# A hybrid decoder block on one core: the next unit's first block product one segment earlier in the down projection

## The chip, the cores and the metric

The program runs on one core of a Trainium2 chip. The core has a matrix engine (PE, with its weight loads shown apart as PEld), a vector engine (DVE), a scalar engine (ACT), a general engine (POOL) and a synchronisation engine (SP); SP and POOL issue the transfers between the chip's memory and the core's SBUF. The matrix engine writes its sums to PSUM, which is divided into banks. The metric is the device time of one execution in microseconds (us); shorter is better.

## The reference

One layer of a decoder block on 512 positions of width 2048, in float32. The part that matters here is the gated MLP at its end: `w_ffn_in` has 2 x 5632 columns, `w_ffn_out` 5632 rows and 2048 columns.

```python
def conv_ffn(h, w_ffn_in, conv_w, conv_b, w_ffn_out):
    S = h.shape[1]
    up = h @ w_ffn_in
    a, b = up[..., :D_FF], up[..., D_FF:]
    a_pad = jnp.pad(a, ((0, 0), (CONV_W - 1, 0), (0, 0)))
    a = (conv_w[0] * a_pad[:, 0:S] + conv_w[1] * a_pad[:, 1:S + 1]
         + conv_w[2] * a_pad[:, 2:S + 2] + conv_b)
    return (jax.nn.gelu(a, approximate=True) * b) @ w_ffn_out
```

Before it come two norms, an input projection, gated linear attention, differential attention and an output projection; after it a norm and a residual sum.

## The kernel before

**Precision.** Each float32 matrix is split into a rounded part (hi) and the rest (lo), and a product is formed as hi x hi + hi x lo + lo x hi, three matmuls. For weights the split is done on the fly. One *granule* is 128 x 1024 weights (512 KB): ACT copies it to hi (line 138), DVE subtracts hi from it to get lo (line 139), and PE reads both. In the down projection the three matmuls stand in lines 1400, 1401 and 1402, in the up projection in lines 1298, 1299 and 1300. The hi and lo pieces lie in a `ring` of three pairs; from the second unit of the down projection on every fourth granule goes to a spare pair `xhi`, `xlo` instead. A piece can be written again only when PE has read it.

**Seven products.** The large projections multiply blocks of 2 x 2 with seven products where the plain way needs eight. A *unit* is one such set of seven, and each product is a *segment* of two granules. A segment of the down projection has 2 x 12 = 24 matmuls of 512 columns. The segments are called x0, z0, y0, z1, x1, y1, y2. The weights that they multiply are:

- x0: block (0,0), loaded by SP into two `rt` buffers, here called t. When x0's split has read t, POOL issues a transfer that *adds* block (0,1) to it in place (`more`, line 1246; line 1506 in the stretch that is ordered by hand).
- z0: t after that addition.
- y0: t after DVE has added block (1,1), called b22, to it (line 1263).
- z1: b22, loaded by SP into `raw` buffers; POOL then adds to it in place in the same way.
- x1: block (1,0), called b21.
- y1: b22 after the addition.
- y2: t after DVE has added b21 to it (line 1281).

The other factor of each product, made of activations, is called a11, s5, s2, s3, a12, s7 and a22 in the same order. For the down projection it is stored in memory by the up projection, loaded by SP into a buffer `st`, and split by ACT (line 151) and DVE (line 152) into its place in `ah` and `al`: this is `prepare`.

**Banks.** x0, y0, y1 and y2 add up in the same PSUM banks (two, one for each 128 rows of output, called j0 and j1 here); after each of them its running sum is read out into the result `acc` by DVE (line 1408) or, in the first two units, partly by ACT (line 1406). z0 and z1 share two other banks, x1 has its own. A later matmul into a bank has to wait until the read of what stands there is done.

**The units.** The up projection has 20 units (plus the first pairs of columns, done plainly), the down projection 10, called d0 to d9 here: five pairs of row groups (index c) by two halves of the columns (cb). Units with an even number start a new c, for which seven new activation factors are prepared. The last row group is done plainly at the end, together with the final norm.

**What sets the order.** From the last three segments of the last up unit to y2 of d0 the order is written out by hand: `change_over` gives the list of segments, `run_in_order` walks through it, makes the granules two or three ahead of their matmuls, and runs hooks (`at`, `prepare_at`) behind each granule. ACT, DVE, PE and POOL keep that order among themselves. From z0 of d1 on, the loop over `downs` states the segments, and a list scheduler in the build, which works with its own estimates of durations, sets the order of the instructions on each engine; it may place an instruction ahead of one that stands earlier in the code. Each engine then works through its own list strictly in order, and so does SP with its transfers. In the loop, x0 of the next unit stands between y1 and y2 of the present one.

Of the kernel before, what the change touches and what calls it, by code (L numbers as in the profile page):

```python
# [35 lines left out]
def hybrid_layer(ctx: ExitStack, tc: tile.TileContext, x, attn_pre_norm, w_in, w_alpha_up, b_alpha,  # L36
# [10 lines left out]
    def dma(o, i):  # L47
        return nc.sync.dma_start(out=o, in_=i)
# [51 lines left out]
    def load(src, a, by=None):  # L100
        raw = wpool.tile([P, GR], F32, name="raw", tag="raw", bufs=4)
        (by or nc.sync).dma_start(out=raw.rearrange("p (a b) -> p a b", a=a), in_=src)
        return raw
# [46 lines left out]
    def split(hi, lo, src):  # L150
        act(hi, src, AF.Copy)  # L151
        tt(lo, src, hi.bitcast(F32), ALU.subtract)
# [10 lines left out]
    def bcast_row(tile_ap, row):  # L163
        dma(tile_ap, row.partition_broadcast(P))
# [960 lines left out]
    def small_tile(name, dt=F32):  # L1125
        return fp.tile([P, GR], dt, name=name, tag="t4", bufs=6)

    def large_tile(name, dt=F32):
        return fp.tile([P, D], dt, name=name, tag="t8", bufs=6)
# [82 lines left out]
    def load_t(src, a):  # L1212
        raw = rp.tile([P, GR], F32, name="rt", tag="rt", bufs=4)
        dma(raw.rearrange("p (a b) -> p a b", a=a), src)
        return raw
# [170 lines left out]
    def piece(v, t, h):  # L1386
        return v[:, t, HK * h:HK * (h + 1), :].rearrange("p k c -> p (k c)")

    def prepare(c, n):
        raw = small_tile("st")  # L1390
        dma(raw, sd[c][n].rearrange("p g x -> p (g x)"))
        split(piece(ah, *place[n]), piece(al, *place[n]), raw)
# [17 lines left out]
    def down_unit(c, cb):  # L1410
        def block(i, j, g):
            gi = 2 * c + 1 + g
            col = 1024 * cb + 512 * j
            return w_y3[:, 4 * gi + 2 * i:4 * gi + 2 * i + 2, col:col + 512]

        def chain(ch):
            return [bank(psa if ch == "y" else psm) for _ in range(2)]

        def out(seg, b):
            for j in range(2):  # L1420
                half, col, sign = {"x0": (0, 0, 1), "z0": (1, 1, 1), "y0": (0, 1, -1), "z1": (0, 1, 1), "x1": (0, 0, 1),
                                   "y1": (1, 1, -1), "y2": (1, 0, 1)}[seg]
                sl = slice(1024 * cb + 512 * col, 1024 * cb + 512 * (col + 1))
                into(acc[2 * half + j][:, sl], b[j], sign, c == 0 and seg in ("x0", "z0", "y0", "y2"))

        return Unit(2, block, down_prods, chain, out, joined=True)
# [21 lines left out]
    downs = [down_unit(c, cb) for c in range(NG // 2) for cb in range(2)]  # L1448
# [4 lines left out]
    def at(u, seg, g, *fs):  # L1453
        hooks.setdefault((u, seg, g), []).extend(fs)

    def load_unit(u):
        u.t = [load_t(u.block(0, 0, g), u.a) for g in range(2)]
        u.b22, u.b21 = [], []

    def load_b(u, name, i, j, by=None):  # L1460
        getattr(u, name).extend(load(u.block(i, j, g), u.a, by) for g in range(2))

    def add_t(u, name, g):
        tt(u.t[g], u.t[g], getattr(u, name)[g], ALU.add)

    def prepare_parts(c, n):
        got = []

        def first():
            got.append(small_tile("st"))  # L1470
            dma(got[0], sd[c][n].rearrange("p g x -> p (g x)"))

        def second():
            split(piece(ah, *place[n]), piece(al, *place[n]), got[0])

        return first, second

    def prepare_at(c, n, load_at, split_at):
        f, g = prepare_parts(c, n)
        at(*load_at, f)  # L1480
        at(*split_at, g)
# [40 lines left out]

    def change_over(u):
        d0, d1 = downs[:2]
        order = [(u, "x1"), (u, "y1"), (d0, "x0"), (u, "y2")]
        order += [(d0, g) for g in ("z0", "y0", "z1", "x1", "y1")] + [(d1, "x0"), (d0, "y2")]
        at(u, "x1", 1, late_tiles)
        prepare_at(0, "s2", (u, "x1", 0), (u, "y1", 0))
        prepare_at(0, "s3", (u, "x1", 1), (d0, "x0", 0))
        prepare_at(0, "s7", (u, "y1", 1), (u, "y2", 0))  # L1530
        prepare_at(0, "a12", (d0, "x0", 0), (d0, "z0", 0))
        prepare_at(0, "a22", (u, "y2", 0), (d0, "y0", 0))
        at(u, "x1", 1, lambda: (add_t(u, "b21", 0), add_t(u, "b21", 1)))
        at(u, "x1", 0, lambda: load_unit(d0))
        at(u, "x1", 0, lambda: load_b(d0, "b22", 1, 1))
        at(u, "y1", 1, lambda: load_b(d0, "b21", 1, 0))
        at(d0, "z0", 1, lambda: load_unit(d1))
        for g in range(2):
            at(u, "y2", g, lambda g=g: add_t(d0, "b22", g))
        at(d0, "z1", 0, lambda: add_t(d0, "b21", 0))  # L1540
        at(d0, "x1", 0, lambda: add_t(d0, "b21", 1))
        for where in ((d0, "z0", 0), (d0, "y0", 0), (d0, "z1", 0), (d0, "x1", 0)):
            at(*where, lambda: late_sums.pop(0)())
        return order

    order = change_over(ups[-1])
    u = ups[-1]
    u.b21 = [load(u.block(1, 0, g), u.a) for g in range(2)]
    for n in ("a11", "s5"):
        prepare(0, n)  # L1550
    with tc.manual_schedule(engines=IN_ORDER):
# [4 lines left out]
    for i, u in enumerate(downs):  # L1556
        if i == 0:
            continue
        nxt = downs[i + 1] if i + 1 < len(downs) else None
        nc_ = (i + 1) // 2  # L1560
        first = i % 2 == 0
        last_cb = i % 2 == 1 and nxt is not None

        if first:
            prepare(i // 2, "s3")
        if i == 6:
            g3 = large_tile("g3")
            bcast_row(g3, ffn_post_norm[0])
        u.y0()
        if first:  # L1570
            prepare(i // 2, "a12")
        u.z1()
        if first:
            prepare(i // 2, "s7")
        u.x1()
        if first:
            prepare(i // 2, "a22")
        if last_cb:
            prepare(nc_, "a11")
        u.y1()  # L1580
        if last_cb:
            prepare(nc_, "s5")
        if nxt is not None:
            nxt.x0()
        if last_cb:
            prepare(nc_, "s2")
        u.y2()
        if nxt is not None:
            nxt.z0()
# [119 lines left out]
```

## Time and profile before

| | us |
|---|---|
| median of 3 runs | 2089.43 |
| lowest and highest | 2087.04 and 2091.67 |
| the profiled execution's own time | 2090.44 |
| its span, first to last instruction | 2088.7 |
| PE busy in the span | 2053.1 |
| DVE busy in the span | 1502.4 |
| ACT busy in the span | 993.8 |
| first matmul of the down projection | 1631.4 from the span's start |

The profile was taken on one execution. Times in views are microseconds from the start of its span. "Busy" of PE counts a matmul until its modelled end, which lies behind the start of the next one, so short pauses do not show in it; the starts of successive matmuls tell more. A row of the timeline gives start, duration, engine, line, operation, what is written and read, and in brackets how long the engine sat idle before it and what ended that.

### The profile page before, as it was taken

The numbers are of one execution on the slowest core, as the hardware profiler recorded it, in microseconds if no ns is written. First come the engines' busy times: TensorE is split into PE (matmuls) and PEld (weight loads), VectorE is DVE, ScalarE is ACT, GpSimd is POOL, SyncE is SP. The second block draws the span as 40 slices with busy tenths as digits, with TensorE's granted clock in tenths as the row PEclk, the third lists the DMA queues.
The fourth block names the chain that finished last, engine by engine and source line by source line (L and its number), as shares of the span: only waits on it lengthen the run. The fifth ranks groups of instructions, "written<-read, shape, count | busy, mean of one in ns | idle before, by whom it ended". The sixth has DMA issues, their size and how long they took to land.

```text
span 2088.7 us, 35508 instructions
## 1 busy us (share of the span) xinstructions
PE 2053.1 (98%) x14417; PEld 1893.3 (91%) x14417; DVE 1502.4 (72%) x1790; ACT 993.8 (48%) x1301; POOL 290.4 (14%) x306
## 2 busy tenths in 40 slices
PE   7999999999999999999999999999999999999997
PEld 6799999999988889899999999999999878787786
DVE  5967777666762265977767777678677778888877
ACT  5544444555552243454454455455455544444443
POOL 0112222222200000011111110111111011111100
PEclk9999999999999999999999999999999999999999
DMA  5488887888883354367577676775777876775753
GB/s 211 124 185 187 196 193 175 192 182 209 193 265 106 93 190 147 98 151 183 133 169 179 143 166 167 163 165 148 187 162 171 249 201 156 198 190 156 180 163 141
DMA packets 281465, 358.61 MB, mean 172 GB/s; under 512 B 14848, under 2 KB 223156, under 8 KB 279380
## 3 DMA queue, kind: packets, MB, share of 16 engines
q1 hardware_dynamic: 192148, 259.85, 37.3%
q0 software_dynamic: 84800, 94.38, 29.9%
q10 hardware_dynamic: 4352, 2.10, 0.4%
q8 instruction: 113, 1.85, 0.3%
q14 instruction: 52, 0.43, 0.1%
HBM read 311.72 MB, written 44.56 MB: 171 GB/s over the span
## 4 chain that ended last, share of the span: by engine, by line
PE 61%; issue 28%; DMA 4%; DVE 3%; POOL 2%; ACT 1%; POOLq 0%; DVEq 0%; SPq 0%; ACTq 0%
PE bank L1300 8%; PE bank L1299 7%; PE bank L1298 7%; PE bank L192 3%; PE bank L193 3%; PE bank L194 3%; PE bank L793 3%; PE bank L795 3%; PE bank L794 3%; PE bank L797 3%; PE bank L798 2%; PE bank L799 2%; PE bank L176 1%; PE bank L174 1%; PE bank L175 1%
## 5 line engine op out<-in xcount | busy, mean ns | idle before, releaser
L138 ACT ACTIVATE ring<-raw 128x1024 fp32r<-128x1024 f32 x315 | 333.1, 1060 | 516.5 <-PE bank L1299 114.1
L139 DVE TENSOR_TENSOR ring<-raw,ring 128x1024 fp32r<-128x1024 f32 x315 | 383.0, 1222 | 270.9 <-ACT ring L138 269.8
L1300 PE MATMUL bank<-ah,ring 128*128 128x256 f32 x1280 | 354.0, 277 | 0.6 <-DVE ring L139 0.5
L1298 PE MATMUL bank<-ah,ring 128*128 128x256 f32 x1280 | 353.9, 276 | 0.0
L1299 PE MATMUL bank<-al,ring 128*128 128x256 f32 x1280 | 353.8, 276 | 0.0
L138 ACT ACTIVATE ring<-rt 128x1024 fp32r<-128x1024 f32 x221 | 233.0, 1059 | 244.0 <-PE bank L1299 135.1
L139 DVE TENSOR_TENSOR ring<-rt,ring 128x1024 fp32r<-128x1024 f32 x221 | 268.7, 1221 | 90.7 <-ACT ring L138 87.3
L1300 PEld LDWEIGHTS bank<-ah,ring 128*128 128x128 f32 x1280 | 240.4, 188 | 1.0 <-DVE ring L139 1.0
L1299 PEld LDWEIGHTS bank<-al,ring 128*128 128x128 f32 x1280 | 240.4, 188 | 0.1
L1298 PEld LDWEIGHTS bank<-ah,ring 128*128 128x128 f32 x1280 | 240.4, 188 | 0.1
L1401 PE MATMUL bank<-ring,ah 128*128 128x512 f32 x424 | 166.6, 393 | 6.7 <-DVE ring L139 6.7
L1402 PE MATMUL bank<-ring,al 128*128 128x512 f32 x424 | 165.4, 390 | 0.0
L1400 PE MATMUL bank<-ring,ah 128*128 128x512 f32 x424 | 158.9, 392 | 0.7 <-ACT ring L138 0.7
L193 PE MATMUL bank<-ring,ah 128*128 128x512 f32 x280 | 109.5, 392 | 0.0
L192 PE MATMUL bank<-ring,ah 128*128 128x512 f32 x280 | 109.4, 396 | 0.0
L194 PE MATMUL bank<-ring,al 128*128 128x512 f32 x280 | 109.1, 392 | 0.0
L1246 POOL DMA_DIRECT2D raw<-in_w_ffn_in_dram x40 | 51.2, 1309 | 398.6 <-DVE ring L139 398.6
L1401 PEld LDWEIGHTS bank<-ring,ah 128*128 128x128 f32 x424 | 79.6, 188 | 27.2 <-DVE ring L139 11.0
L1400 PEld LDWEIGHTS bank<-ring,ah 128*128 128x128 f32 x424 | 79.4, 188 | 19.9 <-ACT ring L138 3.6
L1246 POOL DMA_DIRECT2D rt<-in_w_ffn_in_dram x40 | 51.0, 1295 | 325.3 <-DVE ring L139 302.8
L1402 PEld LDWEIGHTS bank<-ring,al 128*128 128x128 f32 x424 | 79.7, 188 | 16.2
L797 PE MATMUL bank<-ring,ah 128*128 128x256 f32 x320 | 92.0, 288 | 1.9 <-ACT ah L151 1.9
(358 smaller groups left out, 5651.8 us busy)
## 6 DMA issues: line engine op xcount, KB each, us to landing
raw<-in_w_ffn_in_dram SPq DMA_DIRECT2D x96, 512.0 KB, 4.8
raw<-in_w_in_dram SPq DMA_DIRECT2D x56, 512.0 KB, 4.4
raw<-in_w_ffn_out_dram SPq DMA_DIRECT2D x48, 512.0 KB, 6.7
raw<-in_w_in_dram POOLq DMA_DIRECT2D x40, 512.0 KB, 7.1
rt<-in_w_ffn_in_dram SPq DMA_DIRECT2D x40, 512.0 KB, 6.5
rt<-in_w_ffn_in_dram POOLq DMA_DIRECT2D x40, 512.0 KB, 6.2
raw<-in_w_ffn_in_dram POOLq DMA_DIRECT2D x40, 512.0 KB, 6.8
raw<-in_w_o_dram SPq DMA_DIRECT2D x32, 512.0 KB, 4.0
```

Source lines behind the costliest of these rows:

```text
L138: act(hi, raw, AF.Copy)
L139: tt(lo, raw, hi.bitcast(F32), ALU.subtract)
L192: mm(banks[t], ah[:, t, s, :], w[0][:, k, :], start=st, stop=False)
L193: mm(banks[t], ah[:, t, s, :], w[1][:, k, :], start=False, stop=False)
L194: mm(banks[t], al[:, t, s, :], w[0][:, k, :], start=False, stop=sp)
L797: mm(o, sh[:, n, kk, :], wh[:, k, :], start=st, stop=False, **NOW)
L1298: mm(o, wh, sh[:, :, kk, :], start=start and kk == 0 and n == 0, stop=False, **NOW)
L1299: mm(o, wh, sl[:, :, kk, :], start=False, stop=False, **NOW)
L1300: mm(o, wl, sh[:, :, kk, :], start=False, stop=kk == HK - 1, **NOW)
L1400: mm(b[j], sh[:, o:o + P], w[0][:, q, :], start=start and st == 0, stop=False, **NOW)
L1401: mm(b[j], sh[:, o:o + P], w[1][:, q, :], start=False, stop=False, **NOW)
L1402: mm(b[j], sl[:, o:o + P], w[0][:, q, :], start=False, stop=st == 3, **NOW)
```

## The change

The segment x0 of the next unit moves from between y1 and y2 to between x1 and y1. This is done in the loop for every unit, and by hand in the change from the up projection to the down projection (there d0's x0 also moves ahead of the last up unit's y1, and d1's x0 ahead of d0's y1). The hooks that load and split the activation factors move with it, the load of d0's first weights is written ahead of the stretch that is ordered by hand, a11 of the next c is prepared one segment sooner, s5 of the next c ahead of x0 and not behind y1, and a22 between x0 and y1 and not ahead of y1. No instruction is added or taken away.

```diff
@@ def change_over(u):
-        order = [(u, "x1"), (u, "y1"), (d0, "x0"), (u, "y2")]
-        order += [(d0, g) for g in ("z0", "y0", "z1", "x1", "y1")] + [(d1, "x0"), (d0, "y2")]
+        order = [(u, "x1"), (d0, "x0"), (u, "y1"), (u, "y2")]
+        order += [(d0, g) for g in ("z0", "y0", "z1", "x1")] + [(d1, "x0"), (d0, "y1"), (d0, "y2")]
         at(u, "x1", 1, late_tiles)
-        prepare_at(0, "s2", (u, "x1", 0), (u, "y1", 0))
-        prepare_at(0, "s3", (u, "x1", 1), (d0, "x0", 0))
+        prepare_at(0, "s2", (u, "x1", 0), (d0, "x0", 1))
+        prepare_at(0, "s3", (u, "x1", 1), (u, "y1", 0))
...
-        at(u, "x1", 0, lambda: load_unit(d0))
...
     u.b21 = [load(u.block(1, 0, g), u.a) for g in range(2)]
+    load_unit(downs[0])
...
         u.y0()
         if first:
             prepare(i // 2, "a12")
+        if last_cb:
+            prepare(nc_, "a11")
         u.z1()
         if first:
             prepare(i // 2, "s7")
         u.x1()
-        if first:
-            prepare(i // 2, "a22")
-        if last_cb:
-            prepare(nc_, "a11")
-        u.y1()
         if last_cb:
             prepare(nc_, "s5")
         if nxt is not None:
             nxt.x0()
+        if first:
+            prepare(i // 2, "a22")
+        u.y1()
         if last_cb:
             prepare(nc_, "s2")
         u.y2()
         if nxt is not None:
             nxt.z0()
```

The change moves instructions on every engine from there on. Three places of it are shown; rows are instructions in the order in which an engine takes them, with line, operation, tile written, tiles read and size.

**ACT, where the up projection goes over into the down projection.** `raw_16738/16740` are the last up unit's x1, `raw_16620/16622` its y1, `rt_16442/16444` its y2; `rt_16785/16787` before, and `rt_16742/16744` in the change, are d0's t. Before:

```order
L138 ACTIVATE ring_84<-raw_16740 128x1024
L138 ACTIVATE ring_84<-raw_16620 128x1024
L138 ACTIVATE ring_84<-raw_16622 128x1024
L138 ACTIVATE ring_84<-rt_16785 128x1024
L151 ACTIVATE ah_79<-st_16783 128x1024
L138 ACTIVATE ring_84<-rt_16787 128x1024
L138 ACTIVATE ring_84<-rt_16442 128x1024
```

The same place in the change:

```order
L138 ACTIVATE ring_84<-raw_16740 128x1024
L138 ACTIVATE ring_84<-rt_16742 128x1024
L138 ACTIVATE ring_84<-rt_16744 128x1024
L138 ACTIVATE ring_84<-raw_16620 128x1024
L138 ACTIVATE ring_84<-raw_16622 128x1024
L1406 ACTIVATE acc0_16825<-bank_16833 128x512
L1406 ACTIVATE acc1_16826<-bank_16834 128x512
L151 ACTIVATE ah_79<-st_16788 128x1024
L138 ACTIVATE ring_84<-rt_16442 128x1024
```

The two splits of d0's x0 change places with the two of the last up unit's y1; y2 of the up unit now follows its y1 with no other segment between.

**ACT, in the loop, at the end of d3.** `raw_17765/17767` is d3's y1, `rt_17665/17667` before and `rt_17629/17631` in the change its y2; `rt_17909/17911` before and `rt_17877/17879` in the change are t of d4. Before:

```order
L138 ACTIVATE xhi_17036<-raw_17835 128x1024
L138 ACTIVATE ring_84<-raw_17765 128x1024
L151 ACTIVATE ah_79<-st_18013 128x1024
L138 ACTIVATE ring_84<-raw_17767 128x1024
L138 ACTIVATE ring_84<-rt_17909 128x1024
L151 ACTIVATE ah_79<-st_18053 128x1024
L138 ACTIVATE xhi_17036<-rt_17911 128x1024
L138 ACTIVATE ring_84<-rt_17665 128x1024
```

The same place in the change:

```order
L138 ACTIVATE xhi_17036<-raw_17839 128x1024
L138 ACTIVATE ring_84<-rt_17877 128x1024
L151 ACTIVATE ah_79<-st_18013 128x1024
L138 ACTIVATE ring_84<-rt_17879 128x1024
L138 ACTIVATE ring_84<-raw_17765 128x1024
L151 ACTIVATE ah_79<-st_18053 128x1024
L138 ACTIVATE xhi_17036<-raw_17767 128x1024
L138 ACTIVATE ring_84<-rt_17629 128x1024
L138 ACTIVATE ring_84<-rt_17631 128x1024
L138 ACTIVATE ring_84<-rt_17877 128x1024
```

x0's two splits of d4 stood behind both splits of y1, and now stand ahead of them, right behind x1's second one. The last row is already z0 of d4.

**DVE and PE, in the change, around y2 of d3.** `bank_17633/17634` are j0 and j1 of d3's shared banks, `bank_17881/17882` those of d4, `bank_17981/17982` z0 of d4. DVE:

```order
L139 TENSOR_TENSOR ring_84<-rt_17629,ring_84 128x1024
L1408 TENSOR_TENSOR acc0_16825<-acc0_16825,bank_17881 128x512
L1408 TENSOR_TENSOR acc1_16826<-acc1_16826,bank_17882 128x512
L139 TENSOR_TENSOR ring_84<-rt_17631,ring_84 128x1024
L139 TENSOR_TENSOR ring_84<-rt_17877,ring_84 128x1024
L1408 TENSOR_TENSOR acc2_16823<-acc2_16823,bank_17633 128x512
L1263 TENSOR_TENSOR rt_17877<-rt_17877,raw_18017 128x1024
L1408 TENSOR_TENSOR acc3_16824<-acc3_16824,bank_17634 128x512
```

PE, the last matmuls of y1 of d3 and what follows them:

```order
L1402 MATMUL bank_17634<-xhi_17036,al_80 128x512
L1400 MATMUL bank_17981<-ring_84,ah_79 128x512
L1400 MATMUL bank_17982<-ring_84,ah_79 128x512
L1401 MATMUL bank_17981<-ring_84,ah_79 128x512
```

PE does not go from y1 to y2 of d3, though the code states them so: the scheduler puts the whole first granule of d4's z0 (12 matmuls) between them. Then come 12 matmuls of y2 into j0, two of z0's second granule, y2's 12 into j1, and the rest of z0. DVE reads y1's sum out of j0 and j1 (the last L1408 rows) behind the split of that first granule of z0, and between the two stands the addition of b22 to t.

## The prediction

> **What bounds the kernel now.** First the page: PE is busy in 98% of the span, so I read PE.
>
> ```profile
> span 2088.7 us, 35508 instructions
> PE 2053.1 (98%) x14417; PEld 1893.3 (91%) x14417; DVE 1502.4 (72%) x1790; ACT 993.8 (48%) x1301; POOL 290.4 (14%) x306
> ```
>
> The change begins near 1620 us, so all else is left as it is, and the question is what PE loses from there to the end of the down projection. "Busy" hides that. I cut the stretch at the starts of segments, in the view by windows (window, length, PE busy with its matmuls, PEld with its weight loads, then DVE, ACT, POOL, clock, share of the DMA engines, GB/s).
>
> ```profile
> 1642.45:1656.38 13.93, 12.18 (x51) 8.79 (x49) 13.43 (x13) 9.55 (x12) 1.26 (x2) 1.00 0.83 292
> 1678.18:1692.06 13.88, 11.95 (x50) 8.86 (x48) 7.51 (x8) 7.28 (x10) 0.00 (x0) 1.00 0.73 189
> 1708.38:1715.39 7.01, 5.99 (x25) 4.43 (x24) 4.89 (x6) 4.88 (x6) 1.17 (x1) 1.00 0.86 325
> 1726.27:1737.93 11.66, 11.46 (x49) 8.87 (x48) 9.77 (x10) 7.83 (x9) 1.04 (x1) 1.00 0.35 126
> 1803.29:1816.99 13.70, 11.90 (x49) 8.78 (x48) 13.26 (x15) 6.97 (x7) 0.79 (x1) 1.00 0.38 129
> 1816.99:1882.30 65.31, 65.31 (x289) 54.02 (x288) 53.41 (x58) 28.15 (x28) 8.66 (x8) 1.00 0.76 192
> 1882.30:1895.86 13.56, 11.79 (x50) 8.86 (x48) 12.89 (x15) 6.97 (x7) 0.81 (x1) 1.00 0.36 125
> 1955.70:1973.10 17.40, 16.77 (x71) 12.91 (x70) 16.57 (x19) 8.27 (x9) 0.36 (x1) 1.00 0.41 111
> 1973.10:2027.52 54.42, 54.42 (x241) 45.08 (x240) 44.33 (x49) 21.72 (x21) 6.76 (x6) 1.00 0.66 165
> ```
>
> The rows of 288 and 240 weight loads show PE undisturbed: 54.42 / 240 = 0.2267 us a matmul, so 2.72 us a granule and 5.44 us a segment. The clock is full everywhere. The other rows hold two segments each (10.88), the third row one (5.44), the one at 1955.70 three (16.32). They lose:
>
> - d0's z0 and y0: 13.93 - 10.88 = 3.05
> - d0's y2 and d1's z0: 13.88 - 10.88 = 3.00
> - d1's y1: 7.01 - 5.44 = 1.57
> - z0 and y0 of d2, d4, d6: 0.78, 2.82, 2.68
> - d7's y2, d8's z0 and y0: 17.40 - 16.32 = 1.08
>
> Together 14.98 us. Nothing else in the stretch loses more than 0.1. This is all that any reordering of it can win.
>
> Who is late? PE's own waits name the splits, and behind the splits, in ACT's waits (engine, tile, line, releaser: us in total, times, longest), stands a transfer:
>
> ```profile
> PE bank L1401 <- DVE ring L139: 6.7, 9, 1.0
> ACT ring L138 <- DMA rt<-in_w_ffn_out_dram: 59.0, 16, 9.0
> ACT xhi L138 <- DMA rt<-in_w_ffn_out_dram: 12.7, 4, 4.3
> ```
>
> `rt` is t, and the transfer is the addition that POOL issues behind x0 and that z0 needs. ACT and then POOL, in order of time:
>
> ```profile
> 1641.09 1.06 ACT L138 ACTIVATE ring<-rt 128x1024 fp32r<-128x1024 f32 x1 [3.33 <-DMA rt<-in_w_ffn_out_dram]
> 1645.08 1.06 ACT L138 ACTIVATE ring<-rt 128x1024 fp32r<-128x1024 f32 x1 [1.99 <-DMA rt<-in_w_ffn_out_dram]
> 1683.07 1.06 ACT L138 ACTIVATE ring<-rt 128x1024 fp32r<-128x1024 f32 x1 [9.02 <-DMA rt<-in_w_ffn_out_dram]
> 1687.06 2.01 ACT L138 ACTIVATE ring<-rt 128x1024 fp32r<-128x1024 f32 x2 [1.01 <-DMA rt<-in_w_ffn_out_dram]
> 1788.13 1.06 ACT L138 ACTIVATE ring<-raw 128x1024 fp32r<-128x1024 f32 x1 [5.19 <-DMA raw<-in_w_ffn_out_dram]
> 1801.49 1.06 ACT L138 ACTIVATE ring<-rt 128x1024 fp32r<-128x1024 f32 x1 [6.42 <-DMA rt<-in_w_ffn_out_dram]
> 1805.45 1.06 ACT L138 ACTIVATE xhi<-rt 128x1024 fp32r<-128x1024 f32 x1 [2.90 <-DMA rt<-in_w_ffn_out_dram]
> ```
>
> ```profile
> 1630.58 1.17 POOL L1506 DMA_DIRECT2D rt<-in_w_ffn_out_dram  x1 [14.21 <-DVE ring L139]
> 1632.85 1.19 POOL L1506 DMA_DIRECT2D rt<-in_w_ffn_out_dram  x1 [1.10 <-DVE ring L139]
> 1672.77 1.18 POOL L1506 DMA_DIRECT2D rt<-in_w_ffn_out_dram  x1 [15.25 <-DVE ring L139]
> 1675.10 1.19 POOL L1506 DMA_DIRECT2D rt<-in_w_ffn_out_dram  x1 [1.15 <-DVE ring L139]
> 1791.89 1.17 POOL L1246 DMA_DIRECT2D rt<-in_w_ffn_out_dram  x1 [11.81 <-DVE ring L139]
> 1795.35 1.19 POOL L1246 DMA_DIRECT2D rt<-in_w_ffn_out_dram  x1 [2.29 <-DVE xlo L139]
> ```
>
> From issue to the split that waited for it: 10.5 and 12.2 us at d0, 10.3 and 12.0 at d1, 9.6 and 10.1 at d4. From the start of x0 to the start of z0 PE needs two segments, 10.88 us. The additions are issued at about the start of x0 (d4: x0 at 1803.29 - 10.88 = 1792.41, issue at 1791.89), and the split takes ACT 1.06 and DVE 1.2 more. So the stall is a race of about 10 us against 10.9 - 2.0 = 8.9.
>
> **The change, part by part.** No instruction is added, so engine time is not the matter; waits are.
>
> *The hand-written stretch, d0.* Two rows of DVE show when the granules behind x1 are split there now; they are y1's, and the change puts x0's in their place.
>
> ```profile
> 1621.73 1.23 DVE L139 TENSOR_TENSOR ring<-raw,ring 128x1024 fp32r<-128x1024 f32 x1 [0.29 <-ACT ring L138]
> 1624.45 1.23 DVE L139 TENSOR_TENSOR ring<-raw,ring 128x1024 fp32r<-128x1024 f32 x1 [1.50 <-ACT ring L138]
> ```
>
> x0's additions are then issued at about 1623.0 and 1625.7, not 1630.58 and 1632.85. With the same 10.5 and 12.2 us they land at 1633.5 and 1637.9, and z0's granules are wanted on ACT at about 1640 and 1643. The 3.05 go (y0's share too: its additions on DVE stand behind z0's splits). Bounds: 2.2 (z0 alone) to 3.05.
>
> *The hand-written stretch, d1.* Now z0 starts late, by ACT first:
>
> ```profile
> 1684.18 0.50 PE L1400 MATMUL bank<-ring,ah 128*128 128x512 f32 x1 [0.40 <-ACT ring L138]
> ```
>
> In the change x0 is one segment ahead of y1, and z0's first granule comes 10.88 us behind x0, hardly less than the 11.4 of now (d0's y2 starts at 1678.18, x0 5.44 ahead of it at 1672.74, z0 at 1684.18). What moves is the issue: now x0's split waits on ACT behind y1's second granule and its transfer; in the change only the ring's slot holds it, which z1's first granule gives back about 8 us ahead of x0. I take 4 us earlier, more than the 3.00 lost: they go. Bounds 1.2 (only the second granule, which gets 2.72 us more because PE puts y2 ahead of it) to 3.00.
>
> *d1's y1.* Its granule waited for the addition behind z1. It now comes one segment later, 5.44 against 1.57 lost: 1.57 go.
>
> *The loop.* On PE z0's first granule now stands ahead of y2, so from x0 to z0 it is again two segments, 10.88 us. On that count alone the change gives nothing. The win is in ACT's queue: at d3 x0 of d4 stands behind the split of y1's second granule, which sat 5.19 us for its transfer until 1788.13. In the change x0's split comes ahead of it. Its slot is that of z1's first granule, free some 5 us into z1; ACT 1.06 and DVE 1.22 later the addition goes out, 7.5 us from z1's start and 3.4 us ahead of x0's start, where now it is 0.5. With 9.6 us it lands 6.2 us after x0's start against the 8.9 wanted. z0's second granule gains 2.72 us more. So 0.78 + 2.82 + 2.68 + 1.08 = 7.36 go. Bounds: 3 (the issue no earlier, only the second granules gain) and 7.36.
>
> *Added: the eviction.* y2 adds into the banks that y1's sum is read from. In the up unit nothing is between them any more, so PE waits for line 1331.
>
> ```profile
> 1625.99 0.28 PE L1298 MATMUL bank<-ah,ring 128*128 128x256 f32 x1
> 1626.19 0.69 DVE L1329 TENSOR_TENSOR u<-bank,p 128x512 f32<-128x512 f32 x1 [0.51 <-PE bank L1300]
> 1632.47 0.68 DVE L1331 TENSOR_TENSOR u<-u,bank 128x512 f32<-128x512 f32 x1
> 1642.18 1.22 DVE L139 TENSOR_TENSOR ring<-rt,ring 128x1024 fp32r<-128x1024 f32 x1 [4.36 <-ACT ring L138]
> 1643.46 0.50 PE L1401 MATMUL bank<-ring,ah 128*128 128x512 f32 x1 [0.62 <-DVE ring L139]
> ```
>
> y1's first matmul starts at 1625.99, and DVE took up the read of x1 at 1626.19, 0.2 us later; the read lasts 0.68; PE follows DVE's end by 0.06 (1642.18 + 1.22 to 1643.46). That is 0.94, or 2.2 with one split of 1.22 in front. I take 1.0, once. In the loop z0's first granule, 2.72 us, covers the two reads of 0.68 and the 1.22 between them (0.68 + 1.22 + 0.68 = 2.58), and j1 is wanted another 3 us later: 0 there, and 0.9 each for nine units if the cover goes.
>
> The Trainium skill (PSUM — Partial Sum Buffer, section on bank collisions) says the same as the build does here, that PSUM is to be guarded by whole banks and not by addresses. By that rule y2 cannot start on the half that is already read. It leaves the 1.0 as it is and is why the cover in the loop matters.
>
> *b22 and the loads.* The `raw` buffers of the next unit's b22 are those of b21, which no y1 holds, so they are not later. The next b21's are y1's and come 5.4 us later, with three segments and more to spare: 0. a22 is needed a segment behind its place but its buffer and split come far ahead: 0.
>
> *Sum.* 3.05 + 3.00 + 1.57 + 7.36 = 14.98 off, 1.0 on. For residues that I can't place (z0's first granule stays the tightest, nine times) I leave 1.5. Net -12.5: span 2088.7 - 12.5 = 2076.2. Outside the span that execution had 2090.44 - 2088.7 = 1.74, so 2077.9; the median of the runs lies 1.0 below that execution. Forecast 2077.
>
> **The rivals.**
>
> *Half of it.* z0's first granule stays late as its distance on PE is the same; the lower bounds hold: 2.2 + 1.2 + 1.57 + 3 - 2.2 = 5.8 off, 2083.6. For it: PE's new order. Against it: ACT's queue.
>
> *No change.* The transfers are the limit and the waits come back at y1, y0 or the loads. For it: 0.83 to 0.86 of the DMA engines are taken in two of the rows that lose. Against it: 0.35 to 0.41 in four others, and no loss in the row with 0.76. About 2089.
>
> *Slower.* In the change the additions behind z1 and behind x0 go out a segment apart where there were two, with the loads of the next unit among them. If the addition behind x0 takes 3 us longer, z0's first granule is late at every unit, and PE, in order, holds y2 behind it too. The point is a landing later than 8.9 us after x0's start: with the issue 3.4 ahead, 12.3 us; with the issue as now, 9.4. At 15.5 us each of nine boundaries pays 3.2, 29 in all against 15: 2089.4 + 29 - 15 + 1 = 2104; at 14.5, 2095. For it: 12.0 was seen once; against it: 9.6 to 10.1 in the loop.
>
> The Trainium skill (DMA: Bandwidth & Descriptors, section SWDGE vs HWDGE vs iDMA) has each DMA engine take its queues in turn, POOL's among SP's. By that a transfer put among more others lands later, which is this rival's step; no row here shows by how much.
>
> **How the numbers follow.** Forecast 0.64 (2074 to 2081), half 0.17, no change 0.10, slower 0.09. The forecast's own range goes from all 14.98 won with nothing on (2088.7 - 14.98 + 1.74 - 1.0 = 2074.5) to 2081, where half of the loop's 7.36 stays. The 80% range reaches over the half to 2086.5, and down to 2073 since the runs shown spread by 2 us about their median. A difference under 0.2%, 4.2 us, can't be told from no change: the line lies at 2085.25. Faster 0.81, same 0.11, slower 0.08.
>
> **What would show it.** In the new trace the additions behind x0 should be issued 3 to 4 us ahead of x0's first matmul, not 0.5; ACT's wait for `rt` from memory should shrink from 59.0 + 12.7 and PE's for line 139 from 6.7; d0's z0 and y0 should take 10.9, and between the up unit's y1 and y2 there should be one new pause of about 1 us with line 1331 behind it. The prediction is wrong if PE stops at z0's first granule with transfers of 12 us and more, or before y2 with line 1408 behind it.

## The result, and the profile after

The changed kernel takes 2078.03 us (median of 6 runs, 2076.67 to 2079.63) against 2088.78 for the kernel before (6 runs, 2086.67 to 2092.32): a ratio of 0.9944, 95% interval 0.9932 to 0.9956. Forecast were 2077, a range of 2073 to 2086.5, and 0.81 for faster. Ten more runs of the same kernel, made later beside experiments, had medians of 2080.3 and 2080.1; over all 16 the median is 2078.9.

The page of the changed kernel, its span and its engines:

```profile
span 2075.0 us, 35488 instructions
PE 2047.0 (99%) x14417; PEld 1893.9 (91%) x14417; DVE 1507.1 (73%) x1790; ACT 1000.0 (48%) x1301; POOL 290.2 (14%) x306
```

The stretch from the up unit's x1 to the end of the down projection, first of the kernel before, then of the changed one (the view by windows, columns as in the prediction):

```profile
1620.55:2032.96 412.41, 403.31 (x1823) 329.94 (x1822) 337.09 (x354) 190.97 (x198) 47.33 (x40) 1.00 0.70 188
```

```profile
1618.42:2019.84 401.42, 398.03 (x1826) 331.38 (x1824) 340.74 (x354) 196.17 (x198) 47.33 (x40) 1.00 0.71 193
```

The second window holds two weight loads more (1824 against 1822), two matmuls of 0.2267 us. So for the same work the stretch gave 412.41 - 401.42 + 0.45 = 11.44 us. The span fell by 13.7; the other 2.3 lie outside the stretch (it begins 2.13 sooner), in work that the change leaves alone. One execution's span says little about that work: in two later traces of the changed kernel the stretch begins at 1624.53 and 1619.47, and takes 0.6 us more and 0.2 less. Cut at the places that lost before, again by windows:

```profile
1629.39:1636.54 7.15, 5.65 (x50) 5.49 (x48) 5.34 (x6) 5.44 (x6) 0.00 (x0) 1.00 1.03 388
1642.07:1653.32 11.25, 11.25 (x50) 8.86 (x49) 11.25 (x12) 8.09 (x10) 1.26 (x2) 1.00 0.74 250
1675.14:1685.79 10.65, 10.65 (x48) 8.82 (x47) 8.34 (x9) 5.62 (x7) 1.17 (x1) 1.00 0.88 277
1707.55:1712.99 5.44, 5.44 (x25) 4.50 (x24) 3.74 (x6) 2.12 (x2) 0.00 (x0) 1.00 1.06 335
1685.79:1941.47 255.68, 255.68 (x1129) 211.71 (x1128) 220.56 (x232) 126.68 (x126) 31.90 (x27) 1.00 0.71 190
1941.47:1949.12 7.65, 5.75 (x25) 4.42 (x24) 7.65 (x9) 3.07 (x3) 0.00 (x0) 1.00 0.48 147
1949.12:2019.84 70.72, 70.72 (x314) 58.58 (x312) 56.68 (x61) 28.45 (x27) 7.11 (x6) 1.00 0.57 147
```

d0's z0 and y0 (second row) take 11.25 where they took 13.93; d0's y2 and d1's z0 (third) 10.65 where they took 13.88 (the window holds 47 matmuls, one short of two segments, and 47 by 0.2267 is 10.65: nothing is lost); d1's y1 (fourth) 5.44 where it took 7.01. The fifth row is 47 segments in one piece, from d1's y0 to d7's y1: 1128 matmuls by 0.2267 are 255.7, so nothing is lost in it. Besides the 0.37 of the second row two rows still lose: the first, the up unit's y1 (7.15 - 5.44 = 1.71), and the sixth, around d8's z0 (7.65 - 5.44 = 2.21). The waits name both, and ACT's waits no longer contain `rt` from `w_ffn_out` at all; what ACT now waits for most in the down projection is PE:

```profile
PE bank L1401 <- DVE ring L139: 1.9, 1, 1.9
PE bank L1298 <- DVE u L1331: 1.5, 1, 1.5
ACT ring L138 <- PE bank L1402: 123.9, 79, 3.5
```

POOL's rows for the additions behind x0 of d4, d5 and d6, in order of time:

```profile
1774.58 1.17 POOL L1246 DMA_DIRECT2D rt<-in_w_ffn_out_dram  x1 [4.55 <-DVE ring L139]
...
1811.92 1.17 POOL L1246 DMA_DIRECT2D rt<-in_w_ffn_out_dram  x1 [4.95 <-DVE ring L139]
...
1850.74 1.17 POOL L1246 DMA_DIRECT2D rt<-in_w_ffn_out_dram  x1 [4.55 <-DVE ring L139]
```

d1's y0 starts at 1686.02, one matmul behind the edge of the fifth window, and x0 starts 17, 24 and 31 segments of 24 matmuls later, at 1778.50, 1816.58 and 1854.66. (PE takes a few matmuls of a neighbouring segment out of turn, so these starts are counted, not read.) So the additions go out 3.92, 4.66 and 3.92 us ahead of x0; before, counted in the same way, it was 0.74, 2.34 and 0.72. I call this distance the lead.

**The pause at the up unit's y2**, in order of time:

```profile
1634.58 1.22 DVE L139 TENSOR_TENSOR ring<-rt,ring 128x1024 fp32r<-128x1024 f32 x1
1634.77 0.28 PE L1300 MATMUL bank<-ah,ring 128*128 128x256 f32 x1
1635.71 0.68 DVE L1331 TENSOR_TENSOR u<-u,bank 128x512 f32<-128x512 f32 x1
1636.54 0.36 PE L1298 MATMUL bank<-ah,ring 128*128 128x256 f32 x1 [1.50 <-DVE u L1331]
```

y1's last matmul starts at 1634.77; DVE is in a split until the read begins at 1635.71, reads for 0.68, and PE goes on 0.15 later.

**The stall at d8's z0**, SP, ACT, DVE and PE in order of time:

```profile
1928.95 0.34 SPq L48 DMA_DIRECT2D st<-ud  x1
...
1937.23 1.06 ACT L151 ACTIVATE ah<-st 128x1024 fp32r<-128x1024 f32 x1 [3.98 <-DMA st<-ud]
1938.20 2.94 ACT L138 ACTIVATE ring<-rt 128x1024 fp32r<-128x1024 f32 x3
...
1941.80 2.35 DVE L139 TENSOR_TENSOR ring<-rt,ring 128x1024 fp32r<-128x1024 f32 x2
...
1944.21 0.50 PE L1401 MATMUL bank<-ring,ah 128*128 128x512 f32 x1 [1.90 <-DVE ring L139]
```

`ud` holds the operand of the last stage, which is needed some 75 us later. Its split stands in ACT's queue ahead of d7's y2 and d8's z0; its load was issued 8.3 us ahead and ACT waits 3.98 for it. The three splits behind it are late, and PE with them. The kernel before has the same wait at the same place:

```profile
1951.90 1.06 ACT L151 ACTIVATE ah<-st 128x1024 fp32r<-128x1024 f32 x1 [2.31 <-DMA st<-ud]
...
1958.48 1.06 ACT L138 ACTIVATE ring<-rt 128x1024 fp32r<-128x1024 f32 x1 [2.67 <-DMA rt<-in_w_ffn_out_dram]
```

There it is not what holds z0 up: the split of z0's first granule (last row) waits another 2.67 us for the addition. In the changed kernel no such wait comes behind it.

### The profile page after: what moved, and what is told of

The parts are those of the page before. It is cut to its first block, busy times and chain, and to the rows that moved or that the text cites. A ratio compares the mean times of both kernels' runs of the same rounds, so it can differ in the third digit from the quotient of the medians.

```text
span 2075.0 us, 35488 instructions
## 1 busy us (share of the span) xinstructions
PE 2047.0 (99%) x14417; PEld 1893.9 (91%) x14417; DVE 1507.1 (73%) x1790; ACT 1000.0 (48%) x1301; POOL 290.2 (14%) x306
## 4 chain that ended last, share of the span: by engine, by line
PE 67%; DVE 2%; issue 1%; DMA 1%; ACT 1%; POOL 0%; DVEq 0%; POOLq 0%; SPq 0%; ACTq 0%
PE bank L1298 12%; PE bank L1299 12%; PE bank L1300 12%; PE bank L1401 6%; PE bank L1402 6%; PE bank L1400 6%; PE bank L194 3%; PE bank L193 3%; PE bank L192 3%; PE bank L176 1%; PE bank L175 1%; PE bank L174 1%; DVE ring L139 1%; PE bank L1605 0%; PE bank L1606 0%
## 5 line engine op out<-in xcount | busy, mean ns | idle before, releaser
L1401 PE MATMUL bank<-ring,ah 128*128 128x512 f32 x424 | 165.3, 390 | 1.9 <-DVE ring L139 1.9
L1400 PE MATMUL bank<-ring,ah 128*128 128x512 f32 x424 | 152.4, 389 | 0.0
L193 PE MATMUL bank<-ring,ah 128*128 128x512 f32 x280 | 109.6, 393 | 0.0
L192 PE MATMUL bank<-ring,ah 128*128 128x512 f32 x280 | 109.4, 396 | 0.0
```

The source lines that it names most:

```text
L192: mm(banks[t], ah[:, t, s, :], w[0][:, k, :], start=st, stop=False)
L193: mm(banks[t], ah[:, t, s, :], w[1][:, k, :], start=False, stop=False)
L1400: mm(b[j], sh[:, o:o + P], w[0][:, q, :], start=start and st == 0, stop=False, **NOW)
L1401: mm(b[j], sh[:, o:o + P], w[1][:, q, :], start=False, stop=False, **NOW)
```

## The experiments

The theory: z0 stalls when the addition behind x0 lands late, and it was issued late because x0's split stood in ACT's queue behind a split of y1 that waited for memory. The main rival: the gain is PE's new order itself (y1 a segment later, z0's second granule behind half of y2).

### The loop alone, and the change-over alone

Each half of the diff put into the kernel before: lines 1569 to 1590 of the changed kernel, and lines 1523 to 1548.

> The loop as in the change, the hand-written change-over as before. If the places are independent, as the forecast's sum has them: the loop's 7.36 us (d2, d4, d6 and d8) and d1's y1 1.57 go, and the one new stall of the changed kernel's trace (2.06 us at d8's z0, behind a load for the last stage) comes, so -6.9: about 2082 against 2089 before, with 3.05 at d0 and 3.00 at d1's z0 still lost. Rival, that an earlier change-over is what lets the loop run free (PE comes to d2 with its buffers filled): d2, d4 and d6 keep at least half of their 6.28 us, and the time is 2085 or more.

Measured: 2083.02 us (10 runs), ratio 0.9972, 0.9956 to 0.9988. In its trace the loop loses nothing but the stall at d8's z0 (1.8), while d0's z0 and y0 (2.1) and d0's y2 with d1's z0 (4.0) still lose.

> The change-over as in the change, the loop as before. By the forecast's sum: d0's 3.05 and d1's 3.00 go and the pause of 1.66 us between the up unit's y1 and y2 comes, so -4.4: about 2084.4, while d1's y1 (1.57) and the loop's 7.36 stay. With the first run the gains then add up to about the 10.8 us of the whole change. Rival, that the two parts lean on each other: the gains add up to less than 8 us or more than 13 us.

Measured: 2082.76 us (8 runs), ratio 0.9971, 0.9960 to 0.9981. Gains of 5.9 and 6.1 add up to 12.0, more than the 10.8 of both together but within the intervals. By the traces the stretch gains 7.6 and 8.0, 4 us more together than the 11.4 of the whole change. So the halves are not independent: with the loop as before, d1's y1, d2 and d4 lost nothing either, only d6 (1.7) and the stretch around d8 (3.2) did. POOL's rows say why. The additions of d4 and of d6 in this run:

```profile
1784.24 1.17 POOL L1246 DMA_DIRECT2D rt<-in_w_ffn_out_dram  x1 [11.49 <-DVE ring L139]
...
1863.53 1.17 POOL L1246 DMA_DIRECT2D rt<-in_w_ffn_out_dram  x1 [12.18 <-DVE ring L139]
```

x0 starts there at 1788.03 and 1864.23: leads of 3.79 and 0.70. The early change-over hands the loop a lead of 5.2 us at d2, and it wears away from unit to unit (5.2, 4.9, 3.8, 3.2, 0.7).

### The additions held back

The changed kernel, with this in the loop; the second run holds at granule 1 instead of 0. POOL is kept in the program's order there, which moves nothing else on it:

```diff
+    HOLD, waiting = 0, []
+    def release(lo):
+        while waiting:
+            v = waiting.pop(0)
+            w = small.tile([P, 1], F32, name="ms", tag="ms")
+            nc.gpsimd.tensor_scalar(w, lo[:, 0, :1].bitcast(F32), 1.0, 0.0, ALU.mult, ALU.add)
+            v.more(v.t, 1)
...
+                if seg == "y1" and g == HOLD:
+                    release(hl[1])
...
-            self.more(self.t, 1)
+            waiting.append(self)
```

> The changed kernel, with the same order on PE, ACT and DVE, but in the loop POOL issues x0's two additions only once the split of y1's first granule is done (a read of one column of it on POOL stands ahead of them): by the changed kernel's trace at about 0.7 us behind x0's start instead of 3.7 ahead. If the time of issue decides, as the forecast says: they land 8.4 us later, at 9 to 10 us behind x0's start where 8.6 is wanted, and z0's first granule stalls again for 0.5 to 1.5 us in most of eight units: 2082 to 2090. Rival, that the order on PE alone gave the gain (y1 a segment later, the second granule of z0 behind half of y2): no stall comes back, 2078 to 2080.

Measured: 2083.0 us (10 runs), ratio 0.9966, 0.9952 to 0.9980; 4.1 above the 2078.9 of the changed kernel. POOL and ACT at d4 (x0 at 1781.79; the lines are shifted by those inserted):

```profile
1782.28 0.18 POOL L1226 TENSOR_SCALAR ms<-ring 128x1 f32<-128x1 f32 x1 [8.95 <-DVE ring L139]
1782.75 2.43 POOL L1257 DMA_DIRECT2D rt<-in_w_ffn_out_dram  x2 [0.29 <-issue]
...
1796.75 1.06 ACT L138 ACTIVATE xhi<-rt 128x1024 fp32r<-128x1024 f32 x1 [2.03 <-DMA rt<-in_w_ffn_out_dram]
```

The stalls are back at d4, d6 and d8 (3.8, 1.5 and 1.4 us) and nowhere else in the loop, with the order of PE, ACT and DVE the same in the two traces, instruction for instruction.

> As the run before, but the additions wait for the split of y1's second granule, so they go out about 4.1 us behind x0's start. If the time of issue decides, landing is at 12.5 us against 8.6 wanted and every one of eight units loses about 4 us, with PE's waits naming line 139 and ACT's naming rt from memory: 2105 to 2118. This is also the price that the forecast's slower rival put on a late landing (x us late is x us lost, nothing covers it). Rival, that PE's order alone gave the gain: below 2085; or that y2, which stands behind z0's first granule, covers half of it: about 2094.

Measured: 2111.71 us (4 runs), ratio 1.0108, 1.0088 to 1.0128. All eight boundaries stall, 35.3 us in all, with ACT behind PE's wait:

```profile
PE bank L1414 <- ACT ring L138: 18.7, 8, 4.8
```

PE's order is not quite the changed kernel's here: at d4, d6 and d8 PE runs twelve matmuls more, 2.72 us, before it stops for z0. The run held at granule 0, with nothing moved on PE, settles it against PE's order for what it gave back, 4.1 us; this one is the slower rival made real: 33 us for an issue 8 us later.

### The same order as before, with no transfer for y1 to wait on

In the kernel before:

```diff
             self.run("z1", "s3", self.b22)
-            self.more(self.b22, 1)
+            if not extra[0]:
+                self.more(self.b22, 1)
```

> The kernel before, in its old order, but in the loop the additions behind z1 are left out, so y1 multiplies b22 without its second summand and the result differs. y1's split then has no transfer to wait for. If ACT's queue held x0 back, as the forecast says: x0's additions go out about 3 us ahead of x0's start instead of 0.5 (d4 and d6), and the stalls at z0 and y0 of d2, d4 and d6 (6.28 us) go with d1's y1 (1.57) although PE's order is the old one: about 2081. Rival, that the gain of the change came from PE's new order: the issue stays at 0.5 to 2 ahead, z0 still stalls, only d1's y1 goes: about 2087. Fewer transfers also land sooner; so the verdict goes by the times of issue first, and by the total second.

Measured: 2081.31 us (6 runs), ratio 0.9965, 0.9953 to 0.9978. ACT around d4's x0 (1789.97), and POOL:

```profile
1780.49 1.04 ACT L138 ACTIVATE ring<-raw 128x1024 fp32r<-128x1024 f32 x1
1782.01 1.06 ACT L138 ACTIVATE ring<-rt 128x1024 fp32r<-128x1024 f32 x1 [0.48 <-PE bank L1403]
...
1784.63 1.17 POOL L1246 DMA_DIRECT2D rt<-in_w_ffn_out_dram  x1 [34.17 <-DVE ring L139]
```

y1's second split (first row) waits for nothing, x0's follows it, and the addition goes out 5.34 us ahead of x0. The loop loses nothing at all, in the old order of PE. With fewer transfers they also land sooner (the additions to t from d2 on in 7.9 us at the median, not 8.9), so the size of this gain is not the order's alone; the lead is.

The runs put side by side (lead of x0's first addition, PE's loss at that boundary, both us; a lead below zero is an issue behind x0's start; worked out from POOL's and PE's rows as above):

| | d2 | d3 | d4 | d5 | d6 | d7 | d8 | d9 |
|---|---|---|---|---|---|---|---|---|
| before | 1.2, 0.8 | 2.0, 0 | 0.7, 2.8 | 2.3, 0 | 0.7, 2.7 | 2.2, 0 | 1.1, 1.5 | 2.4, 0 |
| changed | 3.8, 0 | 7.4, 0 | 3.9, 0 | 4.7, 0 | 3.9, 0 | 4.7, 0 | 3.9, 2.2* | 4.7, 0 |
| change-over alone | 5.2, 0 | 4.9, 0 | 3.8, 0 | 3.2, 0 | 0.7, 1.7 | 2.3, 0 | 0.7, 3.2 | 2.2, 0 |
| held, granule 0 | -0.5, 0.1 | -0.6, 0 | -1.0, 3.8 | -0.4, 0 | -1.0, 1.5 | -0.4, 0 | -1.0, 1.4 | -0.5, 0 |
| held, granule 1 | -4.5, 6.7 | -3.1, 2.0 | -4.5, 4.1 | -3.6, 5.8 | -4.5, 4.1 | -3.6, 5.6 | -5.0, 2.6 | -3.7, 4.4 |
| y1 unadded | 5.3, 0 | 5.3, 0 | 5.3, 0 | 5.3, 0 | 5.3, 0 | 5.3, 0 | 5.3, 0 | 5.3, 0 |

(* ACT's wait for `ud`, with none for the addition behind it.) In the old order no boundary stalls from a lead of 2.0 on, and all do at 1.2 and less. In the new order some get through at -0.4 to -0.6.

The times of landing, counted here from x0's start, say why. In the old order (first and third row) it is z0's second granule that comes late at d2, d4 and d6; at d4 and d6 its addition goes out 3.5 us behind the first. It landed at most 10.2 us behind x0's start where nothing was lost, and 11.6 to 12.7 behind where PE stalled (d8 apart, where two of z0's first matmuls stand sooner).

In the run held at granule 0 the two additions go out together, half of y2 gives the second granule 2.72 us more, and the first granule decides. Its addition landed at 7.8 to 8.6 us where PE went on, and at 10.1 to 10.8 at d4, d6 and d8. There it took 9.2 to 9.9 us from issue to landing, elsewhere 7.3 to 8.2. The first additions of d3 and of d4 in this run (KB and us to landing):

```profile
rt<-in_w_ffn_out_dram POOLq DMA_DIRECT2D x1, 512.0 KB, 8.0
rt<-in_w_ffn_out_dram POOLq DMA_DIRECT2D x1, 512.0 KB, 9.9
```

Both edges fit the prediction's race: 8.9 us for the first granule, and 8.9 + 2.72 = 11.6 for the second. Why the additions of those three units take longer was not tried.

### y2 directly behind y1 in the loop

The changed kernel, its loop inside `with tc.manual_schedule(engines={ET.PE}):`, so that PE keeps the program's order.

> The changed kernel with PE held to the program's order in the loop, so y2 stands directly behind y1 and all of z0 behind y2. The forecast priced this at 0.9 us for each unit whose cover goes: eight boundaries, +7, about 2085. Upper bound, a split of 1.22 us on DVE ahead of each read as at the up unit (1.66 each): +13, 2091. Rival, that nothing comes: the sum of the first half is complete 1.36 us before y1 ends and that of the second half is wanted 1.36 us later, so a read of 0.94 is hidden; and z0 gets a segment more, so the stall of 2.06 at d8 may go too: 2076 to 2078.

Measured: 2087.38 us (10 runs), ratio 0.9992, 0.9983 to 1.0002. DVE and PE at one of the boundaries:

```profile
1868.10 1.23 DVE L139 TENSOR_TENSOR ring<-rt,ring 128x1024 fp32r<-128x1024 f32 x1 [1.49 <-ACT ring L138]
1869.24 0.68 DVE L1408 TENSOR_TENSOR acc<-acc,bank 128x512 f32<-128x512 f32 x1
...
1870.07 0.47 PE L1400 MATMUL bank<-ring,ah 128*128 128x512 f32 x1 [0.38 <-DVE acc L1408]
```

Each of seven boundaries has pauses of 0.73 (0.54 ahead of the first half, 0.19 ahead of the second); the 1.36 us between the first half's last product and y1's end covers the rest. The first matmuls behind a pause are slower too (0.30 and 0.33 us from start to start instead of 0.2267), so that from x0 to x0 a unit takes 39.04 to 39.08 us where the changed kernel takes 38.08. At d8, where the wait for `ud` was 6.3 us in this order, 5.6 go. So z0's first granule between y1 and y2 is worth 1.0 a unit, a little more than the 0.9 of the forecast.

### The two stalls that are left

> The changed kernel as it is, to stand beside the next two: about 2078, with the pause of 1.7 us at the up unit's y2 and the stall of about 2 us at d8's z0 in its trace. If either is absent or moves, it is no property of the kernel and the next two can't win it.

Measured: 2080.3 us (5 runs), ratio 0.9957, 0.9944 to 0.9971. Both are there, 1.66 and 1.4; and d0's z0 and y0 lost 1.5 in this execution.

In the next run the first half of the last stage's operand is loaded and split in unit 5 (`part(q)` holds the lines that did it behind the loop):

```diff
+        if i == 5:
+            part(0)
         if i == 6:
...
-    for q, at in enumerate(((3, 1), (0, 0))):
...
+    part(1)
```

> The changed kernel, with the load and the split of the last stage's first half issued in unit 5 instead of behind the loop. If the stall of 2.06 us at d8's z0 comes from that load's wait on ACT in front of z0's split: it goes, about 2 us less than the changed kernel beside it, 2076. Rival, that z0's transfer or DVE's long queue is late there anyway: the stall stays at 1 us or more, and the time is within 1 us of the changed kernel.

Measured: 2079.04 us (5 runs), ratio 0.9949, 0.9936 to 0.9963, 1.3 below the run beside it, which is less than the runs spread. The trace is plain: the stall at d8's z0 is gone, 0.2 came at d4.

The next run keeps this and puts the second granule of d0's x0 between the up unit's y1 and y2:

```diff
         gran = [(v, seg, g) for v, seg in order for g in range(2)]
+        gran[3:6] = [gran[4], gran[5], gran[3]]
```

> As the run before, and in the change-over the second granule of d0's x0 stands between the up unit's y1 and y2 instead of ahead of y1. If the pause of 1.66 us at y2 is the read by line 1331 behind a split, its 2.72 us cover it: 1.7 less again, about 2074.5, or 3.7 below the changed kernel. Rival, that the second addition then lands too late for d0's z0 (issued about 8 us later than now, with 10.9 us from there to z0's second granule): up to 2 us come back at z0 and the gain is nothing.

Measured: 2079.25 us (5 runs), ratio 0.9956, 0.9943 to 0.9968: nothing gained. The pause at y2 shrank to 0.66, but d0's z0 lost 4.5 us. Not by the rival: ACT stood before another load that had just been issued (s7's):

```profile
1646.27 1.06 ACT L151 ACTIVATE ah<-st 128x1024 fp32r<-128x1024 f32 x1 [4.85 <-DMA st<-sd0s]
```

So the splits in the change-over were moved away from their loads:

```diff
-        prepare_at(0, "s2", (u, "x1", 0), (d0, "x0", 1))
-        prepare_at(0, "s3", (u, "x1", 1), (u, "y1", 0))
-        prepare_at(0, "s7", (u, "y1", 1), (u, "y2", 0))
+        prepare_at(0, "s2", (u, "x1", 0), (d0, "x0", 0))
+        prepare_at(0, "s3", (u, "x1", 0), (u, "y1", 0))
+        prepare_at(0, "s7", (u, "y1", 1), (d0, "y0", 1))
+        at(d0, "y0", 1, lambda: load_part(0))
+        at(d0, "y1", 1, lambda: split_part(0))
```

> As the run before with both parts moved, but no split on ACT in the change-over stands behind a load that was issued a few us ahead of it: s3's load goes out with s2's, s2 is split behind the first granule of x0, s7 is split behind d0's y0, and the last stage's first half is loaded at d0's y0 and split at its y1. If the stall at d0's z0 of the run before (2.4 us and the slow restart behind it) was ACT waiting 4.85 us for that load: it goes, the pause at the up unit's y2 is below 0.7, d8 has no stall, and the time is 3 us below the changed kernel beside it (2079 to 2076). Rival, that x0's second addition, issued 8 us later than in the change, lands too late for z0: the stall at d0's z0 stays and the time is the changed kernel's.

> The changed kernel beside it, for the difference: 2078 to 2080.

Measured: 2074.06 us (5 runs, 2073.6 to 2075.53), ratio 0.9931, 0.9919 to 0.9944; the changed kernel beside it 2080.09 (5 runs, 2076.66 to 2080.56), ratio 0.9955, 0.9941 to 0.9969. This version beats both kernels: 15 us below the kernel before, 6.0 below the changed one in the same set and 4.8 below its median of 16. The stalls account for 3.4 to 4.1 of that: the stretch takes 400.59 us here and 404.14, 404.74 and 403.95 in the three traces of the changed kernel. The first lines of its waits of PE:

```profile
PE bank L159 <- DVE xt L248: 11.0, 3, 9.7
PE bank L797 <- ACT ah L151: 1.5, 1, 1.5
PE bank L176 <- DVE xlo L139: 0.8, 1, 0.8
```

None of them lies in the stretch of the change any more; one pause of 0.2 us is left there.

## Why the prediction was right, point by point

**The 14.98 us.** The sum was 0.45 short. The row at 1955.70 holds 70 weight loads and not the 72 of three segments, so d8 lost 17.40 - 70 x 0.2267 = 1.53 and not 1.08, and the terms make 15.43. All of them went, but for 0.37 of the 3.05 of d0's z0 and y0 (0.6 and 1.5 in the two later traces); at d8 a new loss came.

**The mechanism** holds in the loop in each step. The lead was put at 3.4 us and measured 3.8 to 4.7 (7.4 at d3); the 0.5 that it was set against is 0.7 by the same count. The time from z1's start to the issue was put at 7.5, and measured 6.96 at d4 (z1 of d3 starts 15 segments behind 1686.02, at 1767.62). That it is ACT's queue and not PE's order was argued from one wait of 5.19 us; the held additions and the unadded y1 show it. For the change-over no run held the additions back: that its 3.05 and 3.00 went by the earlier issue is read from the traces (d1's first addition went out at x0's start and now goes out 4.2 us ahead of it).

**What the forecast left out: the load of `ud`.** It gave this load no term. At d8 of the kernel before, the wait for `ud` had a wait of 2.67 us for the addition behind it, as shown above, so the prediction was right to put that loss to the addition in the main. In the change the addition is there in time, ACT's wait for `ud` has grown to 3.98 us, and it is the last one ahead of z0's splits: 2.21 lost. The early load took this stall away, which shows the cause. The 1.5 us left for residues was meant for z0's first granule, and that is where it fell, by another cause; that it was about the right size is luck.

**The mis-sized term: the eviction.** 1.0 was taken, 1.71 lost. The bounds of 0.94 and 2.2 held. The upper one is a whole split ahead of the read; here 0.83 of one (1634.88 to 1635.71) was ahead. In the loop the cover was said to make it 0, and the trace shows 0.

**The sum.** 14.98 - 1.0 - 1.5 = 12.5 foretold; 15.43 - 0.37 - 1.71 - 2.21 = 11.14 by the terms and 11.44 measured for the stretch. The 0.3 between them are pauses too short for the list, one of them 0.25 in d3's y1.

**The rivals.** "Half" rested on the issue coming no earlier; it came 3 us earlier at d4. Held at the old time or a little behind it, the changed kernel gives 4 us back, so that rival had its price about right. "No change" did not come. "Slower" had the additions land later among more traffic (the 12.0 us that "was seen once" has a 12.2 beside it at d0). Beside the prediction's rule of the Trainium skill (DMA: Bandwidth & Descriptors, section SWDGE vs HWDGE vs iDMA) stand these rows, issues in the stretch with KB and median us to landing, before and changed; nothing in them lands later:

```profile
rt<-in_w_ffn_out_dram POOLq DMA_DIRECT2D x20, 512.0 KB, 9.3
raw<-in_w_ffn_out_dram POOLq DMA_DIRECT2D x20, 512.0 KB, 7.7
rt<-in_w_ffn_out_dram SPq DMA_DIRECT2D x18, 512.0 KB, 7.9
```

```profile
rt<-in_w_ffn_out_dram POOLq DMA_DIRECT2D x20, 512.0 KB, 8.4
raw<-in_w_ffn_out_dram POOLq DMA_DIRECT2D x20, 512.0 KB, 6.1
rt<-in_w_ffn_out_dram SPq DMA_DIRECT2D x18, 512.0 KB, 5.1
```

## What to carry to other kernels

Measure how long ahead of its first reader a chained transfer is issued, place by place: here 1 to 3 us of lead more or less decided between no loss and 1 to 4 us, and nothing in the order of the engine that stalls told it. On an engine that works in order, look for the instruction that waits for memory in front of the one that issues, or lets issue, the next transfer; a load for a much later stage is the easiest to miss and to move. And when the next product goes in between two steps on one bank, move half of it, so that the other half still covers the read (the pause of 1.66 us at the up unit's y2 shrank to 0.66 so, and went once the splits there were moved too).

## What was not expected of the hardware

**A pause costs more than its length.** In the run with the additions held to y1's second granule, PE stood 5 us at d2 and then ran slowly (windows of that run, the third number from the end is the granted clock):

```profile
1716.49:1721.70 5.21, 0.39 (x2) 0.00 (x0) 0.01 (x1) 1.10 (x2) 0.00 (x0) 1.00 1.10 261
1721.70:1725.92 4.22, 4.22 (x12) 3.31 (x12) 4.22 (x5) 1.96 (x2) 0.00 (x0) 0.60 0.37 78
...
1761.00:1766.00 5.00, 3.63 (x15) 2.35 (x15) 3.50 (x4) 1.27 (x2) 0.00 (x0) 1.00 1.07 297
```

For 4.2 us the clock was 0.60 in the mean and a matmul took 0.43 us from start to start instead of 0.2267. Of the 35.3 us of that run about 25 are pauses and about 9 this slow restart, so "x us late is x us lost" was too cheap. It does not go by length alone: a pause of 2.0 us at d4 of the run held at granule 0 (in two parts, with two matmuls between) had it as well,

```profile
1793.83:1799.35 5.52, 4.94 (x13) 3.63 (x14) 5.49 (x6) 2.06 (x3) 0.00 (x0) 0.69 0.68 239
```

while at granule 1 one of 1.8 at d3 (last row of the three, clock 1.00) and one of 2.5 at d8 did not, and one of 2.4 at d4 did. The Trainium skill (TensorE: Matmul & The Clock Gate, Part 1: The HAM clock gate) has the clock halved after an idle window of about 3.4 us that runs free of the program. That equal pauses differ agrees with the free window; the 3.4 does not, since pauses of 2.0 and 2.4 us were enough here. The slow stretch of about 4 us is near the busy window that the page names for the way back.

**Loads landed sooner though no byte was taken away.** The rows above: 7.9 to 5.1 us for the loads of t. Which of the moved transfers makes room for them was not tried.
